# Expert weights in tiles of 2048 columns, smaller gathers outside the branches, and earlier branch announcements

## The chip, the core and the metric

The kernel runs on one core of a Trainium2 chip. The metric is the device time of one execution in microseconds (us); less is better. The core's engines run side by side, each through its own list of instructions in order: PE (TensorE, matrix products; PEld are its weight loads), DVE (VectorE), ACT (ScalarE), POOL (GpSimd) and SP (SyncE, which issues most of the transfers).

## What is computed

The reference is a trunk of two layers on 512 tokens of 1024 channels. Each layer has a mixer (chunked attention, a gated recurrence, a diagonal state-space branch) and a channel mixer: a dense SwiGLU in layer 0, a mixture of experts in layer 1. The change lies in the mixture of experts:

```python
def _swiglu(h, w1, w3, w2):
    return (jax.nn.silu(h @ w1) * (h @ w3)) @ w2

logits = x2.astype(jnp.float32) @ router.astype(jnp.float32)
top_logit, top_e = lax.top_k(logits, TOP_K)       # 2 of 8 experts per token
gates = jax.nn.softmax(top_logit, axis=-1)
...
yb = lax.map(expert_block, (xb, blk_e)).reshape(n_pad, dm)
yb = yb * buf_g[:, None].astype(yb.dtype)
out = jnp.zeros((n + 1, dm), x2.dtype).at[buf_tok].add(yb)
```

An expert's `w1` and `w3` are 1024 x 2816 and its `w2` is 2816 x 1024, all float32.

## The kernel before, in words

Each float32 operand is split into a high and a low float16 part, and a product is three float16 matmuls: high weight by high data (L592), high weight by low data (L593), low weight by high data (L594).

**Weights** come through a stream of units. A unit is a piece of at most 1024 columns, 512 KB. SP loads it into one of 8 `raw` tiles (L210), ACT casts it to its high part `wh` (L219, 8 tiles), DVE makes the low part `wl` as weight minus high part (L232, 6 tiles). `w_get` hands out the next unit, at position `pos`; before that, `w_take` records the casts that are due (`w_ahead`): low parts of all units below `pos + 4` (`AHEAD`), high parts of all below `pos + 6` (`HI_AHEAD`). A load for the unit 8 further is recorded behind each low cast. The order of each engine's list is that in which the code records instructions; nothing moves them afterwards.

**Experts** are sorted by their number of tokens and taken in four pairs, a large one and a small one: `PAIRS`. Which tile sizes a pair uses is chosen on the chip among `VARS[p]`, each choice an unrolled arm of nested branches (`choose`). In this input the first sizes are taken every time: 232 and 56 tokens, 176 and 80, 160 and 112, 136 and 120.

An arm has two phases. In the **up phase**, 22 steps `f`, each for the large and then the small expert, `Expert.up` fetches two units (`w1`, `w3` of 128 rows of the hidden layer), does 48 matmuls on PE, and then evacuates: a SiLU on ACT (L1369), its product with the second half on DVE (`sg`, L1370), a copy on ACT (L1371) and a difference on POOL (L298). In the **down phase**, 8 steps `dt`, `Expert.down` fetches three units (1024, 1024 and 768 columns), does 66 matmuls, and ACT copies the result (`yt`, L1384). `back`, one expert later, transposes it on PE (L1389) and copies it on DVE (`y`, L1393).

Ahead of an arm the tokens of the pair are **gathered** by a product with a 0/1 matrix (`gathers`, L1355), 8 pieces `d` for two experts, eight matmuls each, in columns for the largest size that any arm could need (`TOP`): 328 and 72, 272 and 120, 232 and 128, 176 and 160. ACT and DVE copy the results into `xg`.

Ahead of the gathers the engines are told of the branch to come (`announce`, a branch prefetch hint). Ahead of pair 2 there is another branch, `over`, around a loop for experts with too many tokens; it is not taken here. Half of pair 2's gathers stand in front of it, half behind.

Of the kernel before, what the change touches and what calls it, by code (L numbers as in the profile page):

```python
# [123 lines left out]
def tile_trunk(ctx: ExitStack, tc: tile.TileContext, a: dict, out: bass.AP, dbg=None, upto=99):  # L124
# [69 lines left out]


    units = []
    raws = [cpool.tile([128, 1024], F32, name=f"raw{i}") for i in range(RAW_BUFS)]
    whs = [cpool.tile([128, 1024], F16, name=f"wh{i}") for i in range(WH_BUFS)]
    wls = [cpool.tile([128, 1024], F16, name=f"wl{i}") for i in range(WL_BUFS)]
    W = Ctx()  # L200
    W.n_dma = W.n_hi = W.n_lo = W.pos = W.base = 0

    def w_add(src, n, to=None):
        for o in range(0, n, 1024):
            units.append((src, o, min(1024, n - o), to))

    def w_pump(most=1 << 30):
        while W.n_dma < min(most, len(units)) and W.n_dma - W.n_lo < RAW_BUFS:
            src, o, n, _ = units[W.n_dma]
            SY.dma_start(w_raw(W.n_dma), src(o, n) if callable(src) else src[:, o:o + n])  # L210
            W.n_dma += 1

    def w_raw(u):
        return raws[u % RAW_BUFS][:, :units[u][2]]

    def w_hi():
        u = W.n_hi
        if units[u][3] is None:
            A.activation(whs[u % WH_BUFS][:, :units[u][2]], w_raw(u), AF.Copy, scale=WS)  # L219
        W.n_hi += 1  # L220

    def w_lo(dst=None):
        u = W.n_lo
        if W.n_hi == u:
            w_hi()
        n = units[u][2]
        if dst is None:
            h, lo = whs[u % WH_BUFS][:, :n], wls[u % WL_BUFS][:, :n]
        else:
            h, lo = dst  # L230
            A.activation(h, w_raw(u), AF.Copy, scale=WS)
        V.scalar_tensor_tensor(lo, w_raw(u), WS, h, op0=OP.mult, op1=OP.subtract)  # L232
        W.n_lo += 1
        w_pump()

    def w_ahead(n, nh=0):

        def ok(u, last):
            return u < min(last, len(units)) and units[u][3] is None and u < W.n_dma
        while ok(W.n_lo, min(W.pos + n, W.base + WL_BUFS)):  # L240
            w_lo()
        while ok(W.n_hi, min(W.pos + nh, W.base + WH_BUFS)):
            w_hi()

    def w_take(n=1, ahead=AHEAD, hi=HI_AHEAD, keep=0):

        W.base = W.pos - keep
        w_ahead(n - 1 + ahead, n - 1 + hi)
        r = range(W.pos, W.pos + n)
        assert W.n_lo >= W.pos + n  # L250
        W.pos += n
        return [(whs[u % WH_BUFS], wls[u % WL_BUFS]) for u in r]

    def w_get():
        return w_take()[0]
# [1082 lines left out]
    class Expert:  # L1338
# [10 lines left out]
            return [t[:, i, :self.N] for i in range(2)]  # L1349

        def gather(self, d, oh_, low=V.tensor_copy):
            ps = self.banks()
            for i in range(2):
                for b in range(NB):
                    T.matmul(ps[i], tok[b][:, i, d * 128:(d + 1) * 128], oh_[:, b], start=(b == 0), stop=(b == NB - 1))  # L1355
            A.activation(self.xg[0][:, d], ps[0], AF.Copy)
            low(self.xg[1][:, d], ps[1])

        def up(self, f, get):
            N = self.N  # L1360
            ps = self.banks()
            for m in range(2):
                wh, wl = get()
                for k in range(KD):
                    w = slice(k * 128, k * 128 + 128)
                    mm3(ps[m], wh[:, w], wl[:, w], self.xg[0][:, k], self.xg[1][:, k], k == 0, k == KD - 1)
            sg = sgp()
            gh, gl = self.g
            A.activation(sg[:, 0, :N], ps[0], AF.Silu, scale=OUT_S)  # L1369
            V.scalar_tensor_tensor(sg[:, 1, :N], ps[1], OUT_S * GS, sg[:, 0, :N], op0=OP.mult, op1=OP.mult)  # L1370
            A.activation(gh[:, f], sg[:, 1, :N], AF.Copy)  # L1371
            sub(gl[:, f], sg[:, 1, :N], gh[:, f], P)

        def down(self, dt, get, yt=None):
            N = self.N
            ps = bank()
            for f in range(NF):
                if f % 8 == 0:
                    wh, wl = get()
                c = slice((f % 8) * 128, (f % 8) * 128 + 128)  # L1380
# [123 lines left out]
    def beyond(it):  # L1504
# [17 lines left out]
        def get():  # L1522
# [9 lines left out]
            return t[:, 0], t[:, 1]  # L1532

        for f in range(NF):
            x.up(f, get)
        for dt in range(KD):
            x.down(dt, get)
            x.back(dt, lambda c: y_d[ds(it * 128 + OVB, 128), c])
        V.tensor_scalar(ctr, ctr, 128.0, None, op0=OP.add)


    def pair_last(p, ex):

# [152 lines left out]
        for b in range(NB):  # L1696
# [164 lines left out]
```

## Time and profile before

| | |
|---|---|
| median of 3 runs | 1713.09 us (1712.11 to 1713.91) |
| the profiled execution | 1709.51 us, of which the profile's span is 1707.8 us |
| busy share of the span: PE, DVE, ACT, POOL | 94%, 72%, 59%, 28% |
| matmuls | 18058 |
| mean granted clock of TensorE | 0.965 of full speed |

Times in a profile count from the start of the span. The mixture of experts fills the last half, from about 860 us on. A matmul's recorded duration runs past the start of the next one, since matmuls are pipelined; what one costs in a row of equal ones is the distance of two starts.

### The profile page before, as it was taken

Reading aid. Unit: us, or ns where it says so; the run is one execution under the profiler, and the core shown is the slowest. Engines: PE = TensorE matmul, PEld = TensorE weight load, DVE = VectorE, ACT = ScalarE, POOL = GpSimd, SP = SyncE. Lnnn points to the kernel's source line nnn. Section 1 sums busy time; section 2 is a strip of 40 time slices with the busy share of each in tenths; the row PEclk is TensorE's granted clock in tenths of the full one; section 3 lists DMA queues with packets and bytes.
Section 4 is the critical chain, followed back from the end, with each engine's and each line's share of the span. In section 5 each row is a group of like instructions: output and inputs, shape, how many; then the busy total and the mean of one; then the engine's idle time right before and its main releaser. Section 6 shows DMA issues by size and latency. Waiting matters only on the chain. (4 is left out here: it accounts for less than half of the span.)

```text
span 1707.8 us, 44331 instructions
## 1 busy us (share of the span) xinstructions
PE 1606.6 (94%) x18058; PEld 1205.1 (71%) x18058; DVE 1224.4 (72%) x1720; ACT 1004.8 (59%) x1651; POOL 474.8 (28%) x655
## 2 busy tenths in 40 slices
PE   8959999999999999899799999999989999989985
PEld 4425555445444444455489999999989999989974
DVE  5856664643332245757779987799969998799987
ACT  5444544332322135545478876688858887678875
POOL 6972015930000000301123320233103330123346
PEclk9978899999999999799899999999999999999998
DMA  7312326322342323210189999799978999799994
GB/s 278 109 33 68 96 99 230 108 97 87 113 135 87 126 86 116 62 61 3 49 301 352 348 349 354 266 377 381 386 298 315 379 370 374 284 343 377 378 339 160
DMA packets 123603, 374.57 MB, mean 219 GB/s; under 512 B 30129, under 2 KB 30321, under 8 KB 123362
## 3 DMA queue, kind: packets, MB, share of 16 engines
q1 hardware_dynamic: 96626, 343.00, 55.1%
q10 hardware_dynamic: 21568, 14.24, 2.9%
q0 software_dynamic: 5168, 14.17, 2.3%
q8 instruction: 146, 2.39, 0.6%
q14 instruction: 95, 0.78, 0.1%
HBM read 356.04 MB, written 14.12 MB: 217 GB/s over the span
## 5 line engine op out<-in xcount | busy, mean ns | idle before, releaser
L594 PEld LDWEIGHTS <-wl 128*128 128x128 f16 x4816 | 462.5, 98 | 104.0 <-DVE wl L232 32.7
L232 DVE SCALAR_TENSOR_TENSOR wl<-raw,wh 128x1024 f16<-128x1024 f32 (+1 forms) x374 | 477.3, 1304 | 75.4 <-PE ps L598 51.4
L592 PEld LDWEIGHTS <-wh 128*128 128x128 f16 x4816 | 463.0, 98 | 69.6 <-issue 4.7
L593 PEld LDWEIGHTS <-wh 128*128 128x128 f16 x4816 | 462.3, 98 | 67.1 <-issue 1.6
L594 PE MATMUL ps<-xg,wl 128*128 128x232 f16 (+7 forms) x2816 | 483.3, 222 | 8.4 <-DVE wl L232 7.8
L592 PE MATMUL ps<-xg,wh 128*128 128x232 f16 (+7 forms) x2816 | 483.0, 222 | 1.8 <-issue 1.5
L593 PE MATMUL ps<-xg,wh 128*128 128x232 f16 (+7 forms) x2816 | 483.6, 222 | 0.0
L219 ACT ACTIVATE wh<-raw 128x1024 f16<-128x1024 f32 (+1 forms) x374 | 375.7, 1030 | 130.8 <-PE ps L599 74.2
L298 POOL TENSOR_TENSOR gbuf<-sg,gbuf 128x232 f16<-128x232 f32 (+7 forms) x176 | 180.5, 1026 | 393.4 <-ACT gbuf L1371 393.4
L594 PE MATMUL ps<-gbuf,wl 128*128 128x232 f16 (+7 forms) x1408 | 245.3, 223 | 16.5 <-DVE wl L232 16.5
L592 PE MATMUL ps<-gbuf,wh 128*128 128x232 f16 (+7 forms) x1408 | 245.5, 223 | 0.0
L593 PE MATMUL ps<-gbuf,wh 128*128 128x232 f16 (+7 forms) x1408 | 245.4, 223 | 0.0
L593 PE MATMUL ps<-fl,wh 128*128 128x512 f16 (+1 forms) x368 | 136.2, 370 | 0.7 <-DVE fl L603 0.7
L592 PE MATMUL ps<-fh,wh 128*128 128x512 f16 (+1 forms) x368 | 136.2, 370 | 0.4 <-ACT fh L602 0.4
L594 PE MATMUL ps<-fh,wl 128*128 128x512 f16 (+1 forms) x368 | 136.2, 370 | 0.0
L1371 ACT ACTIVATE gbuf<-sg 128x232 f16<-128x232 f32 (+7 forms) x176 | 55.4, 315 | 80.1 <-DVE sg L1370 80.1
L286 POOL TENSOR_SCALAR rv<-ss 128x1 f32<-128x1 f32 x24 | 5.1, 214 | 348.1 <-ACT u L609 290.9
L232 DVE SCALAR_TENSOR_TENSOR wl<-raw4m,wh 128x1024 f16<-128x1024 f32 (+1 forms) x68 | 97.0, 1426 | 0.2 <-ACT wh L219 0.2
L1165 DVE SCALAR_TENSOR_TENSOR slu<-ps,slu 128x512 f32<-128x512 f32 x22 | 15.2, 692 | 109.3 <-PE ps L594 97.6
L232 DVE SCALAR_TENSOR_TENSOR wl<-raw6m,wh 128x1024 f16<-128x1024 f32 (+1 forms) x68 | 87.6, 1288 | 1.4 <-ACT wh L219 1.4
L592 PE MATMUL ps<-uh,wh 128*128 128x512 f16 x224 | 86.7, 387 | 0.0
L593 PE MATMUL ps<-ul,wh 128*128 128x512 f16 x224 | 86.4, 386 | 0.0
(408 smaller groups left out, 2807.6 us busy)
## 6 DMA issues: line engine op xcount, KB each, us to landing
raw<-mw SPq DMA_DIRECT2D x240, 512.0 KB, 6.1
raw<-fw SPq DMA_DIRECT2D x66, 512.0 KB, 3.9
raw6m<-mw SPq DMA_DIRECT2D x60, 512.0 KB, 6.3
raw7m<-mw SPq DMA_DIRECT2D x60, 512.0 KB, 6.1
raw4m<-mw SPq DMA_DIRECT2D x60, 512.0 KB, 5.9
raw5m<-mw SPq DMA_DIRECT2D x60, 512.0 KB, 6.1
raw<-win SPq DMA_DIRECT2D x36, 512.0 KB, 4.4
raw<-mw SPq DMA_DIRECT2D x32, 384.0 KB, 5.5
```

What stands on the lines that cost most here:

```text
L219: A.activation(whs[u % WH_BUFS][:, :units[u][2]], w_raw(u), AF.Copy, scale=WS)
L232: V.scalar_tensor_tensor(lo, w_raw(u), WS, h, op0=OP.mult, op1=OP.subtract)
L286: P.tensor_scalar(v, ss, inv, EPS, op0=OP.mult, op1=OP.add)
L298: (e or V).tensor_tensor(o, x, y, op=OP.subtract)
L592: T.matmul(ps, wh, xh, start=start, stop=False)
L593: T.matmul(ps, wh, xl, start=False, stop=False)
L594: T.matmul(ps, wl, xh, start=False, stop=stop)
L1165: V.scalar_tensor_tensor(sl, pp[1], OUT_S * GS, sl, op0=OP.mult, op1=OP.mult)
L1371: A.activation(gh[:, f], sg[:, 1, :N], AF.Copy)
```

## The change

In the mixture of experts a unit becomes 2048 columns, 1 MB (both halves of `up`), and in the down phase 1408 columns (11 of the 22 blocks). The pools keep their size: 4 `raw`, 4 `wh` and 3 `wl` tiles of twice the width. The numbers of units that the casts run ahead become 2 and 3, in place of 4 and 6. The dense part keeps units of 1024 columns, as halves of the same tiles. `gathers` outside the arms is cut to the first sizes of `VARS[p]`; an arm with larger sizes gathers the rest itself (`more`). `announce` moves: the first branches of pairs 1 and 3 and the branch `over` are announced after the sixth of eight steps `dt` of the pair in front; all gathers of pair 2 now follow `over`.

```diff
     W.n_dma = W.n_hi = W.n_lo = W.pos = W.base = 0
+    W.size, W.ahead, W.hi = 1024, AHEAD, HI_AHEAD
...
-        for o in range(0, n, 1024):
-            units.append((src, o, min(1024, n - o), to))
+        for o in range(0, n, W.size):
+            units.append((src, o, min(W.size, n - o), to))
...
-    def w_take(n=1, ahead=AHEAD, hi=HI_AHEAD, keep=0):
+    def w_take(n=1, ahead=None, hi=None, keep=0):
 
         W.base = W.pos - keep
-        w_ahead(n - 1 + ahead, n - 1 + hi)
+        w_ahead(n - 1 + (W.ahead if ahead is None else ahead), n - 1 + (W.hi if hi is None else hi))
...
-        w_add(lambda o, n: a["mw2"][ds(es[r], 1), c, :, o:o + n].rearrange("a p c -> p (a c)"), FF)
+        for h in (0, FF // 2):
+            w_add(lambda o, n, h=h: a["mw2"][ds(es[r], 1), c, :, h + o:h + o + n].rearrange("a p c -> p (a c)"), FF // 2)
...
-    for i in range(4, 8):
-        raws[i] = mtile(f"raw{i}m", [1024])
+    raws[:] = raw2[:2] + [mtile(f"raw{i}m", [2048]) for i in range(2)]
+    whs[:], wls[:] = wh2, wl2
+    W.size, W.ahead, W.hi = 2048, 2, 3
...
     def gathers(p, d, low=V.tensor_copy):
-        for i in range(2):
-            n = TOP[i * NP_ + p]
-            Expert(n, xgv(p, i, n), None).gather(d, ohv(p, i), low)
+
+        for i, n in enumerate(VARS[p][0]):
+            Expert(n, xgv(p, i, n), None).gather(d, ohv(p, i)[:, :, :n], low)
+
+    def more(p, n):
+
+        for d in range(KD):
+            for i, m in enumerate(VARS[p][0]):
+                if n[i] > m:
+                    x = [t[:, :, m:] for t in xgv(p, i, n[i])]
+                    Expert(n[i] - m, x, None).gather(d, ohv(p, i)[:, :, m:n[i]])
...
-    w_ahead(2, 2)
+    w_ahead(1, 1)
...
+    def get13():
+        wh, wl = w_get()
+        return [(wh[:, o:o + 1024], wl[:, o:o + 1024]) for o in (0, 1024)]
+
+    def get2():
+        return w_get() + (FF // 256,)
...
                 last = (i, dt)
+            if dt == KD - 3:
+                announce(None if p == 1 else p + 1)
         back(*last)
...
     for p in range(NP_):
 
-        d0 = 0
-        if p == 0:
-            d0 = 4
         if p == 2:
-            announce(n_over > 0, "over")
-            d0 = 4
-            for d in range(d0):
-                gathers(p, d)
             with tc.If(n_over > 0, label="over"):
                 with tc.For_i(0, n_over, 1) as it:
                     beyond(it)
-        announce(ctls[p] > 0, f"pair{p}_0")
-        for d in range(d0, KD):
+        if p % 2 == 0:
+            announce(p)
+        for d in range(4 if p == 0 else 0, KD):
             gathers(p, d, A.copy if p == 0 and d < 6 else V.tensor_copy)
```

What this does to the lists of the engines shows best on DVE. First the up phase of pair 0 in the arm with 232 and 56 tokens, before (`wl<-` is a low cast, `sg<-` the evacuation that waits for PE's last matmul of that expert):

```order
L1370 SCALAR_TENSOR_TENSOR sg<-ps,sg 128x56
L232 SCALAR_TENSOR_TENSOR wl_117<-raw_99,wh_107 128x1024
L232 SCALAR_TENSOR_TENSOR wl_118<-raw_100,wh_108 128x1024
L1370 SCALAR_TENSOR_TENSOR sg<-ps,sg 128x232
L232 SCALAR_TENSOR_TENSOR wl_119<-raw_101,wh_109 128x1024
L232 SCALAR_TENSOR_TENSOR wl_114<-raw4m,wh_110 128x1024
L1370 SCALAR_TENSOR_TENSOR sg<-ps,sg 128x56
```

The same place in the changed kernel:

```order
L1378 SCALAR_TENSOR_TENSOR sg<-ps,sg 128x56
L238 SCALAR_TENSOR_TENSOR wl_106<-raw1m,wh_105 128x2048
L1378 SCALAR_TENSOR_TENSOR sg<-ps,sg 128x232
L238 SCALAR_TENSOR_TENSOR wl_107<-raw_98,wh_102 128x2048
L1378 SCALAR_TENSOR_TENSOR sg<-ps,sg 128x56
```

Two casts between evacuations have become one of twice the width. Before, ahead of the evacuation of an expert at units `pos`, `pos + 1`, the list has casts up to unit `pos + 4`: all of the next expert's two units and the first unit of the one after it. Now, ahead of the evacuation of an expert at unit `pos`, it has casts up to `pos + 1`: the next expert's unit alone.

In the down phase of the same arm, on DVE, before (`y<-` is the copy behind the transposes that PE does after the matmuls of the expert in hand):

```order
L1393 COPY y<-ps 116x2x128
L232 SCALAR_TENSOR_TENSOR wl_119<-raw7m,wh_113 128x1024
L232 SCALAR_TENSOR_TENSOR wl_114<-raw_98,wh_106 128x1024
L232 SCALAR_TENSOR_TENSOR wl_115<-raw_99,wh_107 128x768
L1393 COPY y<-ps 56x128
L232 SCALAR_TENSOR_TENSOR wl_116<-raw_100,wh_108 128x1024
```

and in the changed kernel:

```order
L1403 COPY y<-ps 116x2x128
L238 SCALAR_TENSOR_TENSOR wl_108<-raw1m,wh_105 128x1408
L238 SCALAR_TENSOR_TENSOR wl_106<-raw_98,wh_102 128x1408
L1403 COPY y<-ps 56x128
L238 SCALAR_TENSOR_TENSOR wl_107<-raw_99,wh_103 128x1408
```

Three casts between two copies have become two. Before, the casts ahead of a copy reach three units past the three of the expert in hand; now one unit past its two, which is the first half of the next expert.

## Rows read from the trace of the kernel before

**Rows 1.** The page's head.

```profile
span 1707.8 us, 44331 instructions
```

**Rows 2.** Waits of PE from 860 us on: total us, times, longest.

```profile
PE ps L594 <- DVE wl L232: 24.3, 26, 2.8
PE ps L1355 <- DVEq L1764: 4.5, 1, 4.5
```

**Rows 3.** Windows, up and down phases of pairs 0 to 3: span, busy by engine, clock, DMA.

```profile
core 0: us, PE busy (x) PEld busy (x) DVE busy (x) ACT busy (x) POOL busy (x), PEclk, DMA share, GB/s
860.80:996.20 135.40, 132.90 (x2113) 130.52 (x2114) 125.33 (x154) 106.90 (x175) 43.86 (x42) 1.00 0.92 334
996.20:1064.90 68.70, 68.70 (x1084) 67.75 (x1080) 55.31 (x64) 47.58 (x66) 7.76 (x8) 1.00 0.98 348
1078.80:1200.95 122.15, 121.19 (x2112) 117.30 (x2113) 118.94 (x137) 101.57 (x172) 43.67 (x42) 1.00 0.96 358
1200.95:1262.50 61.55, 61.55 (x1084) 61.26 (x1080) 56.73 (x66) 49.66 (x68) 6.02 (x8) 1.00 1.02 394
1280.90:1406.00 125.10, 125.10 (x2116) 125.01 (x2114) 121.83 (x141) 104.44 (x176) 44.94 (x43) 1.00 0.95 355
1406.00:1470.90 64.90, 64.90 (x1083) 64.74 (x1080) 56.28 (x64) 48.66 (x66) 4.68 (x8) 1.00 1.00 369
1481.30:1607.40 126.10, 121.12 (x2131) 118.65 (x2130) 120.81 (x149) 102.31 (x173) 40.74 (x42) 1.00 0.95 351
1607.40:1695.00 87.60, 71.06 (x1140) 67.97 (x1138) 78.36 (x80) 61.40 (x94) 43.59 (x21) 0.98 0.78 279
```

**Rows 4.** Windows, one step f of the up phase of pairs 0 and 3.

```profile
954.16:960.16 6.00, 6.00 (x103) 5.93 (x99) 5.86 (x8) 4.90 (x9) 2.30 (x2) 1.00 1.00 311
...
1569.14:1574.59 5.45, 5.45 (x101) 5.36 (x98) 5.45 (x7) 4.74 (x9) 2.00 (x2) 1.00 0.93 328
```

**Rows 5.** Timeline of PE in pair 0's up phase: start us, us, what.

```profile
952.82 0.26 PE L594 MATMUL ps<-xg,wl 128*128 128x232 f16 x1
952.92 0.19 PE L592 MATMUL ps<-xg,wh 128*128 128x56 f16 x1
...
954.16 0.26 PE L592 MATMUL ps<-xg,wh 128*128 128x232 f16 x1
```

**Rows 6.** Timeline of ACT and DVE just behind these matmuls.

```profile
953.18 0.36 ACT L1369 ACTIVATE sg<-ps 128x232 f32<-128x232 f32 x1
...
953.58 0.40 DVE L1370 SCALAR_TENSOR_TENSOR sg<-ps,sg 128x232 f32<-128x232 f32 x1
953.89 1.22 DVE L232 SCALAR_TENSOR_TENSOR wl<-raw,wh 128x1024 f16<-128x1024 f32 x1
955.03 1.65 DVE L232 SCALAR_TENSOR_TENSOR wl<-raw4m,wh 128x1024 f16<-128x1024 f32 x1
```

**Rows 7.** Timeline of PE and DVE in pair 0's down phase.

```profile
1028.33 0.26 PE L594 MATMUL ps<-gbuf,wl 128*128 128x232 f16 x1
...
1030.49 0.26 PE L592 MATMUL ps<-gbuf,wh 128*128 128x232 f16 x1
...
1024.94 1.21 DVE L232 SCALAR_TENSOR_TENSOR wl<-raw4m,wh 128x1024 f16<-128x1024 f32 x1
1026.07 0.94 DVE L232 SCALAR_TENSOR_TENSOR wl<-raw5m,wh 128x768 f16<-128x768 f32 x1
1028.74 0.28 DVE L1393 COPY y<-ps 56x128 f32<-56x128 f32 x1 [1.73 <-PE ps L1389]
1028.95 1.20 DVE L232 SCALAR_TENSOR_TENSOR wl<-raw6m,wh 128x1024 f16<-128x1024 f32 x1
```

**Rows 8.** Windows, from the end of pairs 0, 1, 2 to the next arm.

```profile
1064.90:1078.80 13.90, 11.34 (x131) 9.73 (x130) 8.09 (x19) 7.48 (x19) 1.86 (x2) 1.00 0.58 215
1262.50:1280.90 18.40, 12.68 (x131) 11.45 (x130) 6.52 (x18) 5.79 (x17) 1.32 (x2) 0.81 0.43 163
1470.90:1481.30 10.40, 9.69 (x132) 9.38 (x130) 5.81 (x17) 5.57 (x17) 1.20 (x2) 1.00 0.63 247
```

More of the change, by code (lines that the diff above doesn't have):

```diff
@@ L196, in tile_trunk, with halves @@
     units = []
-    raws = [cpool.tile([128, 1024], F32, name=f"raw{i}") for i in range(RAW_BUFS)]
-    whs = [cpool.tile([128, 1024], F16, name=f"wh{i}") for i in range(WH_BUFS)]
-    wls = [cpool.tile([128, 1024], F16, name=f"wl{i}") for i in range(WL_BUFS)]
+    raw2 = [cpool.tile([128, 2048], F32, name=f"raw{i}") for i in range(RAW_BUFS // 2)]
+    wh2 = [cpool.tile([128, 2048], F16, name=f"wh{i}") for i in range(WH_BUFS // 2)]
+    wl2 = [cpool.tile([128, 2048], F16, name=f"wl{i}") for i in range(WL_BUFS // 2)]
+    def halves(ts):
+        return [t[:, o:o + 1024] for t in ts for o in (0, 1024)]
+    raws, whs, wls = halves(raw2), halves(wh2), halves(wl2)
     W = Ctx()
     W.n_dma = W.n_hi = W.n_lo = W.pos = W.base = 0
+    W.size, W.ahead, W.hi = 1024, AHEAD, HI_AHEAD
     def w_add(src, n, to=None):
-        for o in range(0, n, 1024):
-            units.append((src, o, min(1024, n - o), to))
+        for o in range(0, n, W.size):
+            units.append((src, o, min(W.size, n - o), to))
     def w_pump(most=1 << 30):
-        while W.n_dma < min(most, len(units)) and W.n_dma - W.n_lo < RAW_BUFS:
+        while W.n_dma < min(most, len(units)) and W.n_dma - W.n_lo < len(raws):
             src, o, n, _ = units[W.n_dma]
@@ L213, in w_raw @@
     def w_raw(u):
-        return raws[u % RAW_BUFS][:, :units[u][2]]
+        return raws[u % len(raws)][:, :units[u][2]]
     def w_hi():
@@ L218, in w_hi @@
         if units[u][3] is None:
-            A.activation(whs[u % WH_BUFS][:, :units[u][2]], w_raw(u), AF.Copy, scale=WS)
+            A.activation(whs[u % len(whs)][:, :units[u][2]], w_raw(u), AF.Copy, scale=WS)
         W.n_hi += 1
@@ L227, in w_lo @@
         if dst is None:
-            h, lo = whs[u % WH_BUFS][:, :n], wls[u % WL_BUFS][:, :n]
+            h, lo = whs[u % len(whs)][:, :n], wls[u % len(wls)][:, :n]
         else:
@@ L239, in ok @@
             return u < min(last, len(units)) and units[u][3] is None and u < W.n_dma
-        while ok(W.n_lo, min(W.pos + n, W.base + WL_BUFS)):
+        while ok(W.n_lo, min(W.pos + n, W.base + len(wls))):
             w_lo()
-        while ok(W.n_hi, min(W.pos + nh, W.base + WH_BUFS)):
+        while ok(W.n_hi, min(W.pos + nh, W.base + len(whs))):
             w_hi()
-    def w_take(n=1, ahead=AHEAD, hi=HI_AHEAD, keep=0):
+    def w_take(n=1, ahead=None, hi=None, keep=0):
         W.base = W.pos - keep
-        w_ahead(n - 1 + ahead, n - 1 + hi)
+        w_ahead(n - 1 + (W.ahead if ahead is None else ahead), n - 1 + (W.hi if hi is None else hi))
         r = range(W.pos, W.pos + n)
@@ L251, in w_take @@
         W.pos += n
-        return [(whs[u % WH_BUFS], wls[u % WL_BUFS]) for u in r]
+        return [(whs[u % len(whs)], wls[u % len(wls)]) for u in r]
     def w_get():
@@ L1361, in up @@
             ps = self.banks()
-            for m in range(2):
-                wh, wl = get()
+            for m, (wh, wl) in enumerate(get()):
                 for k in range(KD):
@@ L1376, in down @@
             ps = bank()
+            end = 0
             for f in range(NF):
-                if f % 8 == 0:
-                    wh, wl = get()
-                c = slice((f % 8) * 128, (f % 8) * 128 + 128)
+                if f == end:
+                    wh, wl, n = get()
+                    f0, end = f, f + n
+                c = slice((f - f0) * 128, (f - f0) * 128 + 128)
                 gh, gl = self.g
@@ L1520, in beyond, with get1 @@
         ahead = []
-        def get():
+        def get1():
             while jobs and len(ahead) < 2:
@@ L1531, in get @@
             V.scalar_tensor_tensor(t[:, 1, :n], r[:, :n], WS, t[:, 0, :n], op0=OP.mult, op1=OP.subtract)
-            return t[:, 0], t[:, 1]
+            return t[:, 0], t[:, 1], n // 128
         for f in range(NF):
-            x.up(f, get)
+            x.up(f, lambda: (get1()[:2] for _ in range(2)))
         for dt in range(KD):
-            x.down(dt, get)
+            x.down(dt, get1)
             x.back(dt, lambda c: y_d[ds(it * 128 + OVB, 128), c])
         V.tensor_scalar(ctr, ctr, 128.0, None, op0=OP.add)
+    def get13():
[3 more added lines that the diff above has]
+        return w_get() + (FF // 256,)
     def pair_last(p, ex):
@@ L1656, in pair_last @@
             for x in ex:
-                x.up(f, w_get)
+                x.up(f, get13)
             for fn in steps.pop(f, []):
@@ L1665, in pair_last @@
             for i, x in enumerate(ex):
-                x.down(dt, w_get, yt[:, i * n[0]:i * n[0] + n[i]])
+                x.down(dt, get2, yt[:, i * n[0]:i * n[0] + n[i]])
                 for _ in range(2 if dt < KD - 2 else 4):
@@ L1702, in pair_last, with announce @@
             SY.dma_start(out[b * 128:(b + 1) * 128], of[b])
+    def announce(p):
+        label, c = ("over", n_over) if p is None else (f"pair{p}_0", ctls[p])
+        tc.mark_branch_hint_location(label, c > 0, mybir.ALL_ENGINES)
     def pair(p, v):
@@ L1712, in pair @@
             ex.append(Expert(n[i], xgv(p, i, n[i]), g))
+        more(p, n)
         if p == NP_ - 1:
@@ L1716, in pair @@
             for x in ex:
-                x.up(f, w_get)
+                x.up(f, get13)
             if NF - 11 < f < NF - 2:
@@ L1729, in pair @@
             for i, x in enumerate(ex):
-                x.down(dt, w_get)
+                x.down(dt, get2)
                 if last is not None:
```

2 lines of the change are left out of this document (removed).

## The prediction

> **What bounds the kernel now.** First the share of the engines, then the waits, then the stages. The mixture of experts is the part that changes. There PE hardly stops: its waits for a low cast add up to 24.3 us in some 850 [rows 2], and in the eight phases it is busy for nearly every microsecond but in pair 3 [rows 3]. DVE comes close behind, 118.94 of 122.15 us in the up phase of pair 1, and the transfers too, with shares of 0.92 to 1.02 in seven of the eight phases [rows 3]. Two single steps show who sets the pace. In pair 0 a step takes 6.00 us, PE is never idle and DVE is, by 0.14; in pair 3 it takes 5.45 and DVE has 5.45 to do [rows 4]. So the kernel stands on a balance in which the casts are always ready when PE comes to them, and anything that makes PE wait for a cast is paid in full.
>
> **Why a cast is ready now, and will not be.** The lists of DVE above are the heart of this. The evacuation `sg` of an expert waits for PE's last matmul of that expert, and whatever stands behind it in DVE's list waits too. Before, what stands behind it is the second half of the expert two places on, and PE has one and a half experts of weights ahead. In the change it is the whole unit of the expert two places on, and PE has one expert ahead. Each expert's weights can therefore not be ready sooner than this after the last matmul of the expert two places in front: SiLU, product, one cast of 2048 columns.
>
> **The chain in pair 0's up phase.** The last matmul of the large expert starts at 952.82 [rows 5], the SiLU at 953.18, `sg` at 953.58, and the next cast at 953.89 [rows 6]. A cast of 2048 columns isn't in the trace. 1024 columns take 1.21 and 768 take 0.94 [rows 7], so a column costs 1.05 ns, and 2048 take 1.22 + 1024 x 1.05 ns = 2.30 us; the bounds are 2.30 and twice 1.22, or 2.44. The cast ends at 956.19, a chain of 3.37 us. PE meanwhile runs the small expert from 952.92 and would start the next large one at 954.16 [rows 5]. Its first use of a low part is the third matmul: the large expert has 6.00 - 1.24 = 4.76 us for 48 matmuls, 0.099 each, so that is at 954.36. PE waits 1.83 us a step, 22 steps: **40 us**.
>
> The other pairs go the same way. A matmul costs 0.099 / 232 = 0.427 ns a column; PE itself needs 3 large and 48 small matmuls from the last of one large expert to the third of the next. The chain gets a little shorter with the width: if SiLU and product (0.40 and 0.31 at 232) shrank in proportion it would be 3.20 at 176 and 3.08 at 136, if not at all 3.37; I take the middle, 3.28, 3.25 and 3.2.
> Pair 1: PE needs 3 x 0.075 + 48 x 0.034 = 1.87, waits 1.41, a step becomes 48 x 0.109 + 1.41 = 6.66 against 122.15 / 22 = 5.55 [rows 3]: **24 us**.
> Pair 2: 2.50, a wait of 0.75 on a step of 5.69, which PE fills: **16 us**.
> Pair 3: 2.63, a wait of 0.57 on 5.25, so 5.82 against 5.45 [rows 4]: **8 us**. The stalls that bring its phase to 126.10 [rows 3] stay.
>
> **The down phase.** In pair 0 the last large matmul starts at 1028.33, the copy behind the transposes at 1028.74, the next cast at 1028.95, and the next large expert at 1030.49 [rows 7]. Two casts of 1408 columns now stand there, 1.20 + 384 x 1.05 ns = 1.61 us each. The second starts 0.08 before the first has ended, as two casts of 1.22 start 1.14 apart [rows 6], and ends at 1032.09. It is the first half of the next large expert, whose third matmul would come at 1030.69: 1.40 us, 8 times, **11 us**. Pair 1: 3 x 0.075 + 66 x 0.034 and 0.36 for transposes make 2.83 against a chain of 3.76: **7 us**. Pair 2: 3.73, so that cast is in time; the one for the small expert's second half ends 2.23 after the last large matmul, and PE wants it after 1.85: **3 us**. In pair 3 other work (transposes, two scaled copies, sums) takes the copy's place and PE already waits there, 71.06 busy of 87.60 [rows 3]. Nothing shows the new wait. Below it is 0, since DVE with 78.36 is nearly the bound and its work doesn't grow; above it is pair 0's 1.40 for all 16 experts, 22. I take 10, the middle: **10 us**.
>
> **POOL.** The second cast in rows 6 takes 1.65 where the first takes 1.22: POOL's difference runs beside it. Now it would hold up the evacuation behind the cast; pairs 0 and 1 have room there, pairs 2 and 3 less. Between 0 and 0.43 x 44 = 19; I take **4 us**, because the waits above leave DVE some idle time in each step.
>
> [...]
>
> **What is won.** Gathers cost PE 64 matmuls for each column of width they lose: pair 1 goes from 392 to 256 columns, 64 x 136 x 0.427 ns = 3.7 us; pair 2 from 360 to 272, 2.4; pair 3 from 336 to 256, 2.2; pair 0 from 400 to 288, 3.1, of which I count 1.5, as loads and the branch end there too. Pair 1's 13.90 and pair 3's 10.40 [rows 8] are mostly gathers on a busy PE, so they pay out. Ahead of pair 2 PE waits 4.5 us behind the branch `over` [rows 2], and the window's clock is 0.81 [rows 8], which on 12.68 us of matmuls costs about 2.4. An announcement two steps dt ahead (2 x 61.55 / 8 = 15 us [rows 3]) should end most of this; I count 6. Sum **-16 us**.
> Counted at nothing: 1 MB loads (in the slower steps they have more time), wide casts on ACT (4.90 of 6.00 busy [rows 4], and the large expert's SiLU stands behind one that has long ended), fewer instructions on engines that now idle. `more` has nothing to do at these sizes.
>
> **Sum.** 40 + 24 + 16 + 8 = 88, 11 + 7 + 3 + 10 = 31, 4, less 16: **+107 us**. The profiled execution took 1709.5 (its span is 1707.8 [rows 1]), 3.6 under the median of the runs, 1713.1. From the median: **1820 us**, slower by 6%. What a measurement here can tell from no change is about 0.2%, 3 us.
>
> **Rivals.**
> Faster, by the wide cast: if the evacuation did not hold the casts back, DVE would save 2 x 1.22 - 0.08 - 2.30 = 0.06 us an expert, 44 times in the three pairs it paces, 8 us, and the gathers 16: 1713 - 24 = 1689. It decides at a chain shorter than PE's own time to the third matmul. For it speaks that DVE is full in pairs 1 and 3; against it the 3.37 against 1.54 us in pair 0. Chance 0.05.
> [...]
> Less slow: the waits show only in the up phases of pairs 0 and 1, the other chains being shorter than I take them. 1713 + 64 - 16 = 1761. Chance 0.07.
> A slower clock: after the wait at `over` the granted clock fell, 0.81 over that window with PE busy for 12.68 of 18.40, while in pair 3's down phase, 71.06 of 87.60, it was 0.98 [rows 3, 8]. Pair 0's steps would be busy for 6.0 of 7.83, in between. [...] Against it: each single wait is 1.8 us, that one was 4.5. Chance 0.08.
> Announcements lost: the branch comes 15 us or more later, and what was fetched for it may be gone. Then four branches cost 4.5 each, and the 6 are not won: 1820 + 24 = 1844. Chance 0.08.
> [...] Today's announcement within the 13.90 us ahead of pair 1's arm leaves PE 11.34 busy of 13.90 [rows 8], so that one isn't lost.
>
> **Numbers.** The forecast has 0.72. The range leaves out the first three rivals, 0.20: from 1775 (pair 3's down phase and POOL at nothing, chains at their shorter ends and waits about 20 us less) to 1870 (their upper ends, 12 and 15 more, and lost announcements). Slower 0.95, faster 0.04, within 0.2% 0.01.
>
> **What would show it.** Steps of about 7.8, 6.7, 6.4 and 5.8 us in the four up phases; PE's wait for the low cast near 140 us in all, DVE idle ahead of `sg` for PE; a cast of 2.3 us; DMA shares near 0.8; 9 to 10 us between pairs 1 and 2. Steps of 6.0 in pair 0 would prove me wrong.

## The result, and the profile after

The changed kernel takes 1841.58 us (median of 4 runs, 1837.42 to 1843.49), the kernel before 1712.6 beside it: slower by a factor of 1.0769, 95% interval 1.0742 to 1.0796. That is 129 us where 107 were forecast. The profiled execution spans 1841.6 us. In its lines the low cast stands at L238, the high cast at L225, the matmuls at L598 to L600, the evacuation at L1377 to L1379, POOL's difference at L304, the gathers at L1364, the transposes of `back` at L1399.

First the windows: pair 0's gathers, then for each pair its up phase, its down phase and the stretch to the next arm. They answer to [rows 3] and [rows 8].

```profile
core 0: us, PE busy (x) PEld busy (x) DVE busy (x) ACT busy (x) POOL busy (x), PEclk, DMA share, GB/s
850.26:865.45 15.19, 9.85 (x129) 8.82 (x129) 9.81 (x45) 8.90 (x30) 0.00 (x0) 0.90 0.83 330
865.45:1039.15 173.70, 137.35 (x2113) 129.75 (x2114) 112.82 (x110) 101.62 (x130) 88.12 (x42) 0.99 0.69 255
1039.15:1120.57 81.42, 71.45 (x1086) 67.51 (x1081) 55.23 (x48) 47.40 (x50) 8.56 (x8) 1.00 0.87 290
1120.57:1134.41 13.84, 10.06 (x133) 9.54 (x132) 5.84 (x17) 5.87 (x17) 1.87 (x2) 0.75 0.60 240
1134.41:1282.75 148.34, 121.75 (x2118) 117.17 (x2114) 110.26 (x97) 100.78 (x132) 88.99 (x43) 1.00 0.81 295
1282.75:1358.20 75.45, 64.16 (x1084) 61.18 (x1080) 55.25 (x48) 47.28 (x49) 6.52 (x8) 1.00 0.91 317
1358.20:1374.97 16.77, 10.30 (x132) 9.84 (x130) 7.25 (x19) 6.58 (x18) 1.32 (x2) 0.80 0.53 191
1374.97:1515.14 140.17, 128.64 (x2112) 124.45 (x2113) 110.61 (x95) 101.58 (x130) 89.69 (x43) 1.00 0.86 314
1515.14:1585.73 70.59, 66.85 (x1083) 64.72 (x1080) 54.65 (x47) 46.65 (x49) 5.45 (x8) 1.00 0.95 339
1585.73:1596.32 10.59, 7.75 (x132) 7.41 (x130) 7.12 (x18) 6.55 (x19) 1.21 (x2) 1.00 0.77 283
1596.32:1730.68 134.36, 122.58 (x2128) 118.54 (x2129) 112.82 (x108) 101.99 (x131) 84.84 (x43) 1.00 0.89 330
1730.68:1827.95 97.27, 72.75 (x1125) 68.38 (x1122) 71.03 (x58) 59.94 (x77) 50.38 (x22) 0.96 0.73 255
```

Difference to the same stretch before, and what was forecast for it, in us:

| | pair 0 | pair 1 | pair 2 | pair 3 | sum | forecast |
|---|---|---|---|---|---|---|
| up phase | +38.3 | +26.2 | +15.1 | +8.3 | +87.9 | 40 + 24 + 16 + 8 = 88 |
| down phase | +12.7 | +13.9 | +5.7 | +10.7 | +43.0 | 11 + 7 + 3 + 10 = 31 |
| stretch behind the pair | -0.1 | -1.6 | +0.2 | | -1.5 | -3.7 - 8.4 - 2.2 = -14.3 |

Pair 3's down phase is taken to its last expert matmul in every run. Before, that one ends at 1693.94 (PE, timeline),

```profile
1693.72 0.22 PE L594 MATMUL ps<-gbuf,wl 128*128 128x120 f16 x1
```

so the phase took 86.5 us; the window of 87.60 in [rows 3] runs 1.1 us past it.

Pair 0's gathers took 15.63 us before, so -0.4 (forecast -1.5). They also begin later, at 850.26 in place of 845.17, in a part whose work is the same. In nine of the ten profiles of the experiments below, with wide and narrow units, they begin between 840.4 and 847.2, in one at 849.9, so this is no effect of the change; phases are compared from here on, not spans alone.

Now one step of pair 0's up phase, PE, then ACT, then DVE, beside [rows 5] and [rows 6]:

```profile
951.09 0.26 PE L600 MATMUL ps<-xg,wl 128*128 128x232 f16 x1
...
952.43 0.26 PE L598 MATMUL ps<-xg,wh 128*128 128x232 f16 x1
952.52 0.26 PE L599 MATMUL ps<-xg,wh 128*128 128x232 f16 x1
954.50 0.27 PE L600 MATMUL ps<-xg,wl 128*128 128x232 f16 x1 [1.71 <-DVE wl L238]
...
951.44 0.36 ACT L1377 ACTIVATE sg<-ps 128x232 f32<-128x232 f32 x1 [2.42 <-PE ps L600]
...
951.84 0.40 DVE L1378 SCALAR_TENSOR_TENSOR sg<-ps,sg 128x232 f32<-128x232 f32 x1 [2.65 <-ACT sg L1377]
952.16 2.28 DVE L238 SCALAR_TENSOR_TENSOR wl<-raw,wh 128x2048 f16<-128x2048 f32 x1
```

Read it as a chain: last large matmul 951.09, SiLU 951.44, product 951.84, cast 952.16 to 954.44, third matmul of the next large expert 954.50. That is 3.41 us where 3.37 were forecast; the cast takes 2.28 for 2.30. PE has run two matmuls of the next large expert and then stands for the low part. ACT stands 2.42 us for PE, and DVE 2.65 us for ACT's SiLU: nobody is busy for long, all wait in a circle. From 845 us on PE's waits for the low cast are 129.4 us, against 24.3 in [rows 2] and some 140 forecast:

```profile
PE ps L600 <- DVE wl L238: 129.4, 132, 3.2
PE ps L1399 <- ACT yt L1394: 8.4, 3, 3.4
PE ps L1364 <- ACTq L1787: 3.4, 1, 3.4
```

The second line is one that the forecast lacked; the third is the wait behind the branch `over`, which it expected to be nearly gone. In pair 1's down phase the same chain isn't alone (ACT, DVE, PE, timeline):

```profile
1328.60 1.38 ACT L225 ACTIVATE wh<-raw0m 128x1408 f16<-128x1408 f32 x1 [2.56 <-DMA raw0m<-mw]
...
1330.00 1.62 DVE L238 SCALAR_TENSOR_TENSOR wl<-raw0m,wh 128x1408 f16<-128x1408 f32 x1 [2.52 <-ACT wh L225]
...
1331.69 0.25 PE L600 MATMUL ps<-gbuf,wl 128*128 128x176 f16 x1 [1.33 <-DVE wl L238]
```

The high cast waits for its transfer, the low cast for the high one, PE for the low one. And at the end of pair 0 (ACT and PE, timeline):

```profile
1122.16 1.91 ACT L225 ACTIVATE wh<-raw1m 128x2048 f16<-128x2048 f32 x1 [2.32 <-DVE wl L238]
1123.98 0.20 ACT L1394 ACTIVATE yt<-ps 128x56 f32<-128x56 f32 x1
...
1124.23 0.41 PE L1399 MATMUL ps<-cst,yt 128*56 128x128 f32 x1 [3.41 <-ACT yt L1394]
```

with the windows of this wait and of the gathers behind it:

```profile
1120.57:1125.00 4.43, 0.67 (x4) 0.15 (x3) 2.21 (x3) 2.02 (x2) 1.32 (x1) 0.77 1.00 422
1125.00:1128.60 3.60, 3.58 (x34) 3.58 (x34) 0.74 (x3) 0.87 (x3) 0.55 (x1) 0.50 0.89 342
```

A copy of 0.20 us, the pair's last, stands on ACT behind a high cast of the next pair that starts late. PE waits 3.41 us with nothing else to do, and then runs the first gathers at a granted clock of 0.50 over 3.60 us. What shorter gathers had saved is gone there.

### The profile page after: what moved, and what is told of

Its sections match the earlier page's. It is cut to its first block, busy times and chain, and to the rows that moved or that the text cites. A ratio compares the mean times of both kernels' runs of the same rounds, so it can differ in the third digit from the quotient of the medians.

```text
span 1841.6 us, 42606 instructions
## 1 busy us (share of the span) xinstructions
PE 1623.7 (88%) x18058; PEld 1203.1 (65%) x18058; DVE 1175.6 (64%) x1480; ACT 988.6 (54%) x1411; POOL 659.0 (36%) x655
## 5 line engine op out<-in xcount | busy, mean ns | idle before, releaser
L600 PEld LDWEIGHTS <-wl 128*128 128x128 f16 x4816 | 463.7, 98 | 229.2 <-DVE wl L238 158.6
L600 PE MATMUL ps<-xg,wl 128*128 128x232 f16 (+7 forms) x2816 | 484.6, 222 | 86.3 <-DVE wl L238 86.2
L598 PEld LDWEIGHTS <-wh 128*128 128x128 f16 x4816 | 464.5, 98 | 78.3 <-ACT wh L225 6.5
L238 DVE SCALAR_TENSOR_TENSOR wl<-raw,wh 128x1024 f16<-128x1024 f32 (+2 forms) x254 | 446.1, 1770 | 88.4 <-PE ps L604 51.4
L598 PE MATMUL ps<-xg,wh 128*128 128x232 f16 (+7 forms) x2816 | 483.9, 222 | 3.5 <-issue 2.6
L304 POOL TENSOR_TENSOR gbuf<-sg,gbuf 128x232 f16<-128x232 f32 (+7 forms) x176 | 360.3, 2047 | 292.3 <-ACT gbuf L1379 292.3
L225 ACT ACTIVATE wh<-raw 128x1024 f16<-128x1024 f32 (+2 forms) x254 | 358.2, 1427 | 154.5 <-PE ps L605 74.2
L600 PE MATMUL ps<-gbuf,wl 128*128 128x232 f16 (+7 forms) x1408 | 249.2, 224 | 44.0 <-DVE wl L238 43.3
L598 PE MATMUL ps<-gbuf,wh 128*128 128x232 f16 (+7 forms) x1408 | 249.6, 223 | 5.5 <-ACT wh L225 5.5
L599 PE MATMUL ps<-gbuf,wh 128*128 128x232 f16 (+7 forms) x1408 | 249.4, 223 | 0.0
L238 DVE SCALAR_TENSOR_TENSOR wl<-raw0m,wh 128x2048 f16<-128x2048 f32 (+1 forms) x76 | 158.9, 2091 | 19.4 <-ACT wh L225 18.9
L238 DVE SCALAR_TENSOR_TENSOR wl<-raw1m,wh 128x2048 f16<-128x2048 f32 (+1 forms) x76 | 152.4, 2006 | 20.3 <-issue 14.8
L1378 DVE SCALAR_TENSOR_TENSOR sg<-ps,sg 128x232 f32<-128x232 f32 (+7 forms) x176 | 52.4, 298 | 137.7 <-ACT sg L1377 132.8
L225 ACT ACTIVATE wh<-raw1m 128x2048 f16<-128x2048 f32 (+1 forms) x76 | 127.3, 1675 | 22.7 <-DMA raw1m<-mw 15.1
L598 PE MATMUL ps<-fh,wh 128*128 128x512 f16 (+1 forms) x368 | 136.1, 370 | 0.4 <-ACT fh L608 0.4
L600 PE MATMUL ps<-fh,wl 128*128 128x512 f16 (+1 forms) x368 | 136.1, 370 | 0.0
L225 ACT ACTIVATE wh<-raw0m 128x2048 f16<-128x2048 f32 (+1 forms) x76 | 127.2, 1674 | 10.4 <-DMA raw0m<-mw 10.2
L1377 ACT ACTIVATE sg<-ps 128x232 f32<-128x232 f32 (+7 forms) x176 | 48.2, 274 | 116.5 <-PE ps L600 114.7
```

The source lines that it names most:

```text
L225: A.activation(whs[u % len(whs)][:, :units[u][2]], w_raw(u), AF.Copy, scale=WS)
L304: (e or V).tensor_tensor(o, x, y, op=OP.subtract)
L598: T.matmul(ps, wh, xh, start=start, stop=False)
L599: T.matmul(ps, wh, xl, start=False, stop=False)
L600: T.matmul(ps, wl, xh, start=False, stop=stop)
```

## The experiments

Each ratio below is to runs of the kernel before beside that experiment (medians 1707 to 1709 us). The phases are read from one profile of each kernel.

**The lead alone (how many units the casts run ahead), on the changed kernel.**

```diff
-    W.size, W.ahead, W.hi = 2048, 2, 3
+    W.size, W.ahead, W.hi = 2048, 3, 4
```

> The changed kernel with one number pair altered: casts run 3 units ahead (high parts 4) in place of 2 and 3; units stay 2048 columns, gathers and announcements stay as changed. Theory (the lead): the up phases lost 38.4 + 26.3 + 15.1 + 8.3 = 88 us and most of the 43 us of the down phases because only one expert of weights was cast ahead of the evacuation; with two ahead the steps go back to 6.00, 5.55, 5.69 and 5.45 us, PE's waits for the low cast from 129 us to under 35, and the time to 1700 to 1730. Rival 1 (width): a cast or a transfer twice as long is itself the cost; then the steps stay above 7 us in pair 0 and the time above 1800. Rival 2 (raw tiles): the up phases recover but the down phases keep their 43 us, because a 1408-column piece leaves a third of each 2048-column raw tile unused: 1755.

1754.93 us, 1.0266 of the kernel before (1.0234 to 1.0297). Up phases of pairs 0 to 3, then the down phases of pairs 0 and 1:

```profile
859.56:995.52 135.96, 134.17 (x2114) 131.38 (x2114) 114.68 (x111) 102.00 (x132) 87.69 (x42) 0.99 0.89 326
1086.58:1209.63 123.05, 120.14 (x2120) 117.76 (x2117) 109.00 (x97) 98.97 (x131) 87.87 (x42) 1.00 0.91 348
1307.19:1432.31 125.12, 125.12 (x2115) 125.11 (x2116) 110.08 (x95) 101.32 (x130) 89.27 (x43) 1.00 0.93 348
1518.30:1644.57 126.27, 120.44 (x2131) 118.69 (x2132) 111.02 (x108) 98.17 (x130) 83.11 (x43) 1.00 0.92 343
...
995.52:1070.34 74.82, 70.26 (x1078) 67.03 (x1075) 53.83 (x46) 46.03 (x49) 8.56 (x8) 1.00 0.91 313
1209.63:1282.37 72.74, 63.94 (x1077) 61.21 (x1075) 53.72 (x47) 45.99 (x48) 6.82 (x8) 1.00 0.93 333
```

86 of the 88 us of the up phases are back, with casts and transfers as wide as in the change. So width is not the price there, the lead is. The down phases keep 31 of their 43 us. That the time meets the second rival's 1755 to the microsecond is luck: the rival kept all 43, and what the down phases gave back, and more, was lost in the stretches behind pairs 0, 1 and 2, which took 16.24, 24.82 and 15.30 us, 13.7 more than in [rows 8].

**The lead alone, on the kernel before:** low casts 3 units of 1024 columns ahead in place of 4.

```diff
-    def w_take(n=1, ahead=AHEAD, hi=HI_AHEAD, keep=0):
+    def w_take(n=1, ahead=None, hi=HI_AHEAD, keep=0):
...
+    W.ahead = 3
```

> The kernel before, with one number altered in the mixture of experts: low casts run 3 units ahead in place of 4, so that, as in the change, only the next expert's weights are cast ahead of an evacuation, but in two casts of 1024 columns. Theory (the lead, with the chain of the prediction): the first half is ready one cast of 1024 sooner than the wide one, so PE waits 3.37 - 1.08 - 1.54 = 0.75 us a step in pair 0 and 3.28 - 1.08 - 1.87 = 0.33 in pair 1, nothing in pairs 2 and 3: steps of 6.75, 5.88, 5.69, 5.45; with some 4 to 8 us in the down phases 1735 to 1748. Rival (width alone): no step changes, 1713.

1771.91 us, 1.0373 (1.0342 to 1.0403), well above the 1735 to 1748 expected: the lead costs with narrow casts too, but far more than the chain. Pair 0's step is 6.82 (6.75 expected), and its up phase takes 152.70 us, 17 more than before. Pairs 1 to 3 are uneven and lose 14, 10 and 12 us. To see why, the same kernel with its transfers cut:

```diff
-            SY.dma_start(w_raw(W.n_dma), src(o, n) if callable(src) else src[:, o:o + n])
+            m = n if W.n_dma < W.full else n // 8
+            SY.dma_start(w_raw(W.n_dma)[:, :m], src(o, m) if callable(src) else src[:, o:o + m])
```

> The kernel before with the lead of 3 units of 1024 columns (as in that run), and from the ninth unit of the mixture of experts on each transfer brings an eighth of its columns (the rest of the weights is left out; the casts read what the tile held before). That run lost 14, 10 and 11 us in the up phases of pairs 1 to 3, where the chain gave 7, 0 and 0. Theory (late transfers: a tile comes free one cast later, the high cast waits for its transfer on ACT, and the SiLU behind it): with the transfers cut the steps become even, 6.8 in pair 0, about 5.9, 5.7 and 5.45 in pairs 1 to 3, and the up phases about 152, 130, 125 and 123 us; about 1740. Rival (the order on DVE alone): pairs 1 to 3 stay uneven, at 135 to 138 us.

1727.73 us (2 runs; about 1740 expected). Up phases of pairs 1 and 2 with whole transfers:

```profile
1102.90:1239.20 136.30, 122.69 (x2114) 117.51 (x2114) 121.35 (x139) 105.36 (x173) 44.28 (x43) 1.00 0.92 325
1319.00:1454.20 135.20, 129.79 (x2119) 125.07 (x2117) 122.78 (x141) 105.74 (x176) 44.88 (x43) 1.00 0.92 328
```

and with an eighth of them:

```profile
1098.55:1223.80 125.25, 121.93 (x2113) 117.22 (x2114) 120.15 (x139) 104.47 (x173) 44.10 (x43) 1.00 0.17 47
1302.48:1428.90 126.42, 125.23 (x2116) 124.95 (x2113) 122.09 (x141) 105.92 (x176) 44.89 (x43) 1.00 0.17 47
```

Pair 0 stays at 152.47 (152.70 with whole transfers): that is the chain. Pairs 1 and 2 lose their unevenness, and pair 3 goes from 137.75 to 125.26: that was transfers. A shorter lead also frees the `raw` tiles later, since a load waits for the low cast of the unit that held its tile (SyncE's queue waits 81.8 us for low casts in pair 1's up phase of the kernel before). In that phase ACT's high casts wait 10.4 us for transfers with the lead of 3, and 0.4 in the kernel before.

**Transfers in the changed kernel's down phase.**

```diff
+            m = n // 8 if n == FF // 2 else n
```

> The changed kernel with the transfers of the down phase cut: each brings 176 of its 1408 columns, and the casts read what the tile held before in the others (this part of the weights is left out). Theory: in the down phase of pairs 1 and 2 the high cast waits for its transfer (some 21 us of ACT's idle time each) and the low cast behind it, so with the transfers gone these phases go from 75.5 and 70.6 us to about 68 and 67, pair 0's stays near 80, and the time falls by 10 to 15 us. Rival (the chain alone, with the copy behind the transposes): the down phases stay as they are, within 3 us in all.

1817.58 us, 1.0648 of the kernel before in place of 1.0769, so some 21 us less than the changed kernel (10 to 15 expected). Down phases of pairs 0 to 3, and the stretch between pairs 0 and 1:

```profile
1031.13:1112.38 81.25, 71.28 (x1086) 67.62 (x1081) 54.29 (x48) 46.75 (x51) 8.55 (x8) 1.00 0.27 82
1271.07:1340.08 69.01, 63.30 (x1084) 61.27 (x1080) 54.63 (x48) 45.44 (x50) 6.50 (x8) 1.00 0.30 89
1497.05:1564.61 67.56, 66.18 (x1083) 64.81 (x1080) 54.59 (x48) 45.10 (x49) 5.44 (x8) 1.00 0.31 93
1708.08:1798.78 90.70, 71.41 (x1125) 67.54 (x1122) 72.41 (x58) 59.76 (x77) 52.79 (x22) 0.96 0.26 76
...
1112.38:1121.69 9.31, 7.69 (x132) 7.27 (x131) 5.54 (x17) 5.09 (x17) 1.86 (x2) 1.00 0.75 265
```

In pairs 0 to 2 what is left over the kernel before, 12.6, 7.5 and 2.7, is the chain. What went in pairs 1 and 2, 6.4 and 3.0 us, was late transfers. One such phase varies by some 2 us from profile to profile (72.93 and 72.44 in place of 75.45 and 70.59 in the run without POOL's difference below), but the two together hardly do: 145.4 and 146.0 us with whole transfers, 136.6 here. Pair 3 can't be parted in this way. There 4.2 us are left over the kernel before and 6.6 went, but the phase with narrow pieces and the old leads gets shorter without its transfers too, from 84.80 to 82.11 us in the two runs with mixed units below; over that, 8.6 are left. The stretch behind pair 0 shrank by 4.5 us too, its clock back at 1.00: there the wait for the last copy was the transfers' as well.

**Wide units in the up phase, pieces of 1024 in the down phase** (lead of 3 wide units there, the old leads here, two pieces to a tile).

```diff
     def ld13(r, f):
+        W.size = 2048
...
     def ld2(r, c):
+        W.size = 1024
...
+        wide = hs(W.pos + 1) - hs(W.pos) == 2
+        w_ahead(n - 1 + ((6 if wide else AHEAD) if ahead is None else ahead), n - 1 + ((8 if wide else HI_AHEAD) if hi is None else hi))
```

> The changed kernel with units of 2048 columns in the up phases alone, casts there 3 units ahead, and in the down phases pieces of 1024, 1024 and 768 columns again, each in half a tile, with the leads of the kernel before; gathers and announcements stay as changed. Theory (lead, and raw tiles filled to two thirds): up phases as in the run with the lead of 3 (136.0, 123.1, 125.1, 126.3 us), down phases as before (68.7, 61.5, 64.9, 86), the stretches between pairs as in the run with the small parts alone; all in all 1696 to 1704, a ratio of 0.992 to 0.997. Rival (something else in the changed stream costs in the down phases, such as high casts further ahead on ACT): down phases above 70 us in pairs 1 and 2, and 1720 or more.

1720.44 us, 1.0055 (1.0025 to 1.0085), half a miss: 1696 to 1704 were expected. The down phases are back at 68.66, 61.50, 64.90 and 84.80 us, as expected. The up phases of pairs 1 and 2 aren't as in the run with the lead of 3, but 135 us, and the runs spread from 1702 to 1727. One late transfer there (ACT, then DVE, timeline of pair 2):

```profile
1345.98 1.91 ACT L235 ACTIVATE wh<-raw 128x2048 f16<-128x2048 f32 x1 [0.96 <-DMA raw<-mw]
1347.80 0.28 ACT L1388 ACTIVATE sg<-ps 128x160 f32<-128x160 f32 x1
...
1348.12 0.33 DVE L1389 SCALAR_TENSOR_TENSOR sg<-ps,sg 128x160 f32<-128x160 f32 x1 [1.23 <-ACT sg L1388]
```

The SiLU stands behind a high cast that waits for its transfer, so the evacuation is late and every cast behind it. A load of 1 MB landed 6.9 to 7.1 us after its issue here and 5.9 to 6.1 in the run with the lead of 3 (medians by tile); why it is slower here stays open. With the transfers cut in the same way as above:

> The run with 2048 columns in the up phases and pieces of 1024 in the down phases, its transfers cut to an eighth in the same way (that part of the weights is left out). That run lost 13 and 10 us in the up phases of pairs 1 and 2. Theory (late transfers): these phases go to 22 x 5.36 = 118 and 22 x 5.68 = 125 us, pair 3's to about 119, and the time to about 1685; then a cast of 2048 columns costs nothing by itself, and where DVE was the bound, with steps of 5.5, it gains 0.1 us a step. Rival (the wide casts hold up the evacuations whatever the transfers do): pairs 1 and 2 stay above 130.

1684.8 us (2 runs), as expected. Up phases of pairs 1 and 2, and the down phase of pair 3:

```profile
1068.36:1190.05 121.69, 119.72 (x2117) 119.50 (x2114) 112.50 (x99) 102.66 (x135) 87.86 (x43) 0.99 0.18 49
1263.10:1389.40 126.30, 125.13 (x2112) 124.96 (x2113) 113.04 (x98) 103.28 (x134) 88.34 (x43) 1.00 0.18 48
...
1586.01:1668.12 82.11, 68.58 (x1124) 66.10 (x1121) 74.71 (x72) 58.13 (x91) 41.97 (x20) 0.99 0.28 81
```

Pair 1's steps are 5.36 from the third on, where they were 5.55 on average before and 5.64 in the run with narrow casts, a lead of 3 and cut transfers. DVE is busy for 112.50 us of this phase, 118.94 before. So the wide cast does save DVE time, if the transfers let it; the first two steps, 7.80 and 6.69, take most of it back (121.69 us for the phase, 118 expected).

**The small parts alone, on the kernel before:** gathers, `more` and announcements as in the change, units as before.

> The kernel before, with units of 1024 columns and its leads as they were, and of the change only the smaller gathers, the rest gathered in the arms, and the moved announcements. Theory (as forecast): the shorter gathers give 10 us and the branch named over 6, so 1697. Rival: the gathers pay out, the announcement does not (in the changed kernel PE still waited 3.4 us behind that branch, and 4.5 before), and the gathers behind it run at the lower granted clock: 1702 to 1708. If what ate the gain in the changed kernel is its wide high cast in front of the last copy of a pair, the stretch between pairs 0 and 1 is about 3.7 us shorter here (10.2 in place of 13.9).

1699.98 us, 0.9946 (0.9922 to 0.9969), 9 us faster, the lowest median of a complete version here, between the theory's 1697 and the rival's 1702. Stretches behind pairs 0, 1 and 2:

```profile
1069.69:1079.43 9.74, 7.66 (x131) 7.38 (x131) 6.06 (x18) 5.59 (x18) 1.87 (x2) 1.00 0.81 310
1264.53:1279.80 15.27, 9.71 (x132) 9.24 (x130) 6.68 (x20) 5.62 (x18) 1.32 (x2) 0.89 0.51 196
1469.69:1478.63 8.94, 7.63 (x132) 7.37 (x130) 5.18 (x17) 5.40 (x18) 1.20 (x2) 1.00 0.68 262
```

Against [rows 8] that is -4.2, -3.1 and -1.5, for gathers and announcements together. Pair 0's gathers give nothing, 15.91 us against 15.63.

**Gathers alone, and the announcement of `over` taken away.** The first leaves `announce` and the order of pair 2's gathers as before; the second is the kernel above with

```diff
-                announce(None if p == 1 else p + 1)
+                if p != 1:
+                    announce(p + 1)
```

> The kernel before with the smaller gathers alone (the rest gathered in the arms); announcements and the place of pair 2's gathers as before. Theory (the announcements are worth nothing): as much faster as the run with both, a ratio of 0.993 to 0.997, about 1701. Rival (the forecast's split, 10 us for gathers and 6 for the branch named over): the branch's part is missing here, and the time is 3 to 6 us above the run with both.

> The small parts alone (as in the run with both) without the announcement of the branch named over; the others stay. Theory (that announcement brings nothing): the stretch between pairs 1 and 2 stays at 15.3 us, PE's wait behind the branch at 3.8, and the time at the ratio of the run with both, 0.995. Rival (it brings part of the fetch): the wait grows by 2 us or more and the stretch with it, 1702 to 1706.

1702.29 us, 0.9964 (0.9949 to 0.9979), and 1704.26 us, 0.9982 (0.9964 to 1.0001). The intervals overlap each other and that of the run with both. With the gathers alone the stretches behind pairs 0 and 2 take 11.85 us, at a granted clock of 0.86, and 9.01: -2.1 and -1.4 against [rows 8]. The stretch between pairs 1 and 2 takes 15.27 us with the announcement two steps `dt` ahead, 16.49 with it half of the gathers ahead, and without it

```profile
1255.41:1274.56 19.15, 9.78 (x132) 9.32 (x130) 6.78 (x20) 5.71 (x18) 1.32 (x2) 0.82 0.41 153
```

with PE's wait behind the branch, in the list of waits, at

```profile
PE ps L1355 <- PEq L1771: 6.3, 1, 6.3
```

in place of 3.8 and 3.5. That looks like some 3 us of waiting for the announcement, but these are single profiles, and the other runs don't bear it out: with the same announcement two steps ahead this wait was 3.4 us in the changed kernel, 7.8 in the run with the lead of 3 and 7.2 without POOL's difference. What announcing `over` is worth stays open.

**POOL's difference left out of the changed kernel.**

```diff
-            sub(gl[:, f], sg[:, 1, :N], gh[:, f], P)
+            if not self.zero:
+                sub(gl[:, f], sg[:, 1, :N], gh[:, f], P)
```

> The changed kernel without POOL's difference in the up phase (the low half of the hidden layer is left out: POOL fills it with zeros once a pair, at its start). In the changed kernel one difference takes 2.05 us in place of 1.03, and the prediction put 4 us (between 0 and 19) on its holding up the evacuations. Theory (the waiting is POOL's own, and no evacuation or cast is later for it): the up phases stay at 173.7, 148.3, 140.2 and 134.4 us within 1 us each, and the time within 3 us. Rival (the forecast's term): the casts and evacuations come sooner, the up phases of pairs 2 and 3 shrink by 1 us or more each, and the time by 4 to 19 us.

1842.4 us. The up phases are 173.09, 147.59, 140.07 and 134.85, each within 0.8 us of the changed kernel's. POOL's doubled time costs nothing here: 1842.4 us without it, 1841.58 with it.

## Why the prediction was right, and where it was off

**The up phases: right, term by term.** 87.9 us against 88; steps of 7.88, 6.70, 6.37 and 5.86 against 7.83, 6.66, 6.43 and 5.82. The mechanism is shown from both sides: a longer lead takes nearly the whole loss back, a shorter one puts such a loss, 17 us in pair 0, into the kernel before, and the chain read from four rows had the right length.

**The down phases: the chain right, transfers left out.** The run with cut transfers leaves 12.6, 7.5 and 2.7 for pairs 0 to 2, where 11, 7 and 3 were forecast. For pair 3 it leaves between 4.2 and 8.6, where I took 10, the middle of 0 and 22, without a row for it. The step that failed is "Counted at nothing: 1 MB loads (in the slower steps they have more time)". Late transfers cost 6.4 + 3.0 = 9.4 us in pairs 1 and 2, where the kernel before stood at DMA shares of 1.02 and 1.00 [rows 3], and between 2.1 and 6.6 in pair 3. A piece lands no later than before once it is issued (medians of 5.4 to 5.6 us for 704 KB, 5.9 to 6.3 for the 512 KB before); it is issued later: in pair 1's down phase SyncE's queue waits 47.4 of 75.45 us for a low cast to free a tile, against 30.6 of 61.55 before. My reading is that room is what they lacked: a piece of 1408 columns holds a tile of 2048, so four tiles take 5632 columns of the down phase, where eight tiles took 7509 (eight pieces of 939 on average). With pieces of 1024 and the old leads the phases went back; with the longer lead and pieces of 1408 they kept 31 of 43 us. How much of it is room and how much lead was not tried apart.

**What is won: forecast 16, measured 2.** With narrow units the stretches behind pairs 0 and 2 give 4.2 and 1.5 with gathers and announcements, 2.1 and 1.4 with gathers alone, where 3.7 and 2.2 were forecast for the gathers. In the changed kernel the pair's last copy behind a late high cast of the next pair (3.41 us of waiting behind pair 0), and the clock after that wait (0.50 over 3.60 us), take it back. For the branch `over` I counted 6 us. The wait behind it was 4.5 before and is 3.4 in the changed kernel, so 1 of the 6 came; with waits from 3.4 to 7.8 behind the same announcement, no run shows what it gives.

**POOL: forecast 4, measured 0.** The difference takes 2.07 us (median) in place of 1.03, but the longer time is its own. Beside the cast of 952.16 to 954.44 above (POOL, timeline):

```profile
952.75 2.17 POOL L304 TENSOR_TENSOR gbuf<-sg,gbuf 128x232 f16<-128x232 f32 x1 [3.41 <-ACT gbuf L1379]
```

165 of the 176 casts of 2048 columns run beside such a difference and take 2.28 us (median, 2.33 at most); the eleven others take 2.28 to 2.29. In the run that leaves the difference out DVE is busy for 110.12 and 110.58 us in the up phases of pairs 1 and 2, against 110.26 and 110.61 here. Of the differences, those beside a wide cast take 2.10 us (median), the last two of each up phase, beside none, 1.32 to 1.50; what makes the others longer was not shown.

Together: 88 + 43 - 2 = 129, as by the medians, against 88 + 31 + 4 - 16 = 107.

**The rivals.** The wide cast is cheaper, as "faster" had it, and by more than its 0.06 us. Undisturbed, two casts of 1024 take 2 x 1.22 - 0.08 = 2.36 us, one of 2048 takes 2.28. But beside POOL's difference the second narrow cast takes 1.65 [rows 6] (1.47 in the median of those that start while a difference runs, 1.22 of the others), and the wide one doesn't grow: in the up phases of pairs 1 and 2 DVE's busy time fell from 118.94 and 121.83 us [rows 3] to 110.26 and 110.61, or 0.20 and 0.26 for each expert in each step. The changed kernel got nothing for it, since the evacuation did hold the casts back. The clock stayed at 0.99 to 1.00 in the up phases, with PE busy for 137.35 of 173.70 us in pair 0, so "slower clock" fell. "Less slow" fell with the 15.1 and 8.3 us of pairs 2 and 3. The announcements for pairs 1 and 3 were not lost: PE goes from the last gather to the arm's first matmul within 0.1 us.

## What to carry to other kernels

What counted in DVE's in-order list was how much is cast ahead of an instruction that waits for PE: one more wide unit ahead took back 86 of 88 us in the up phases. Merging two units into one of twice the size and halving the counts keeps the bytes but shortens that lead from one and a half experts to one; work out the chain, last use to next ready (3.41 us in pair 0), against what PE still has to do (1.54 us). A buffer of fixed tiles holds less when a piece does not fill its tile (5632 columns in place of 7509), and the late transfer above shows two engines further on, as 2.56 us on ACT, 2.52 on DVE and 1.33 on PE. A gain in one stretch is only kept if the engine is waited for there in the new kernel too: behind pair 0 the shorter gathers ended at 13.84 us, 13.90 before. And a wait read from one profile needs a second one before it prices anything; behind the branch `over` it went from 3.4 to 7.8 us.

## What was not expected of the hardware

A wait of 3.41 us of PE at the end of pair 0 was followed by gathers at a granted clock of 0.50 over 3.6 us, while the waits in its up phase, 23 of up to 1.7 us, left the clock at 0.99. And the time of the kernel with wide units in the up phase alone scatters: 1702 to 1727 us, where each of the three kernels with small parts and narrow units, 12 runs apiece, spreads over 9 to 16 us. That its late transfers are the reason is likely but not shown. Nor was a wait behind the branch `over` expected that goes from 3.4 to 7.8 us with the same announcement ahead of it.
